# A hybrid RWKV-7 / S5 / PEER block on one core: the gather stream runs on through its two buffers instead of stopping at its tenth row

## The chip, the core and the metric

The kernel runs on one core of a Trainium2 chip. The core has a matrix engine (PE, with its weight loads shown as PEld), a vector engine (DVE), a scalar engine (ACT), a general engine (POOL) and a queue that issues plain transfers (SP). Each engine takes its instructions strictly in the order of the program. The metric is the device time of one execution in microseconds; lower is better.

## What is computed

One pre-norm residual layer over 1024 tokens of width 1024, in float32. Shortened:

```python
xn = rms_norm(x); p = xn @ w_in
y_a = rwkv7_time_mix(p[...])            # 8 heads x 64, a recurrence over the tokens
y_b = s5_ssm_glu(p[...])                # diagonal complex SSM, GELU, GLU
h = x + (sigmoid(g_a) * y_a + sigmoid(g_b) * y_b) @ w_out
# PEER, by blocks of 128 tokens: 8 heads, 16 of 128*128 single-neuron experts each
q = (xt @ wq); s = einsum(q, subkeys); sv, si = top_k(s, 16)
e, gate = best 16 of the 16 x 16 sums     # 128 experts for each token
hid = gelu(einsum('td,thkd->thk', xt, table_u[e]))
h = h + einsum('thk,thkd->td', gate * hid, table_v[e])
out = rms_norm(h)
```

## The kernel before

The tokens are eight blocks of 128. All blocks go through the projections, the S5 part, the RWKV recurrence and the mix into `h`; for the expert part they are split. Blocks 1 to 5 (`DB`) are **dense**: for them a gate table over all 16,384 experts is built with one-hot matmuls (tiles `oha`, `ohb`, `gm`, function `gate_table`), and then all experts are multiplied through, chunk by chunk of 128 experts (`dense_steps`: score matmuls into `S`, value matmuls into `acc`, weights `u` and `v` streamed from memory and split in high and low parts `uh`, `ul`, `vh`, `vl`). Blocks 0, 6 and 7 (`GB`) are **gathered**: for each of their 3 x 128 = 384 rows (one expert per token and row), POOL issues one indirect transfer of 128 x 2048 floats, a megabyte, into a buffer `row`. Then DVE takes the dot product with the token (`row<-row,gx`) and reads the sum out (`hid`), ACT takes the GELU and multiplies with the gate, and DVE adds the value half into the accumulator (`gacc<-row,hid,gacc`). The selection of a block (the `top16` and `combine` instructions `tv`, `ti`, `t`, `cv`, `ci`, `oh`) runs on DVE and partly on POOL. Blocks 6 and 7 (`LATE`) are selected only during the dense stage, in `late_steps`.

No order of instructions is written out. Fourteen streams (front, pre, state, mix, top, table, gather, dense, late and others, listed at line 2020) run as coroutines. A planner (`Weave`, lines 50 to 350) keeps a time line of its own for every engine with modelled durations, takes the operation that could start first by that time line, and among the operations that could start on that engine at that time the one with the highest bonus (`run`, line 260). The gather stream has the lowest bonus of the streams ahead of the dense stage, -1.0 (line 1994), so it gets the gaps that the planner sees. What the planner emits is the fixed order of each engine's program. Where an operation may go to DVE or POOL (`either`), the planner also chooses the engine.

The gather stream (`gather_stream`, line 1988) starts when block 0 is selected. At that time it has two `row` buffers. Until the flag `dense` it runs with `keep` = 1, that is, it takes the dot and the sum of row n-1 once row n is issued; after the flag it has a third buffer (later five), and it is spread evenly over the dense stage (`step`). At row number `GE` = 10 it waits for the flag `dense`, which the dense stream sets when the gate tables are complete (line 1964). The other flags are `mixed` (line 1898: the first six blocks are mixed; the table stream waits for it) and `tables`. Row 128 needs the selection of block 6.

Nearly all instructions are recorded on one line, L171, of the planner's `issue`; so the rows of the profile are told apart by their tiles.

Of the kernel before, what the change touches and what calls it, by code (L numbers as in the profile page):

```python
# [37 lines left out]
NG, ND = len(GB), len(DB)  # L38
# [336 lines left out]
class Kern:  # L375
# [1393 lines left out]
    def build(self, ctx, out):  # L1769
# [14 lines left out]
        NP = LATE[0] // 2  # L1784
        sc = [[] for _ in range(NP)]
        self.rings = {}
        GE = 10
        wv = self.weave
        E = mybir.EngineType
        X = {}  # L1790
# [197 lines left out]
        def gather_stream():  # L1988
            wv.wait(lambda: GB[0] in sel and "glu" in flags)
            wv.cur.kb = 2.0  # L1990
            self.padd, self.keep = 8, 1
            n, N, at, end = 0, 128 * NG, 0.0, 0.99
            RLT = 1.2
            wv.cur.bonus = -1.0
            for n in range(128 * NG + 1):
                if n == N:
                    break
                if n >= GE:
                    wv.wait(lambda: "dense" in flags)
                if "dense" in flags:  # L2000
                    self.padd = 0
                    self.keep = len(self.rings["row"]) - 1
                    step = (end - at) / (N - n)
                    if "late" not in flags:
                        step /= RLT
                    at = max(at + step, X["part"] - 2 * step)
                    wv.wait(lambda: X["part"] >= min(at, 2.0))
                b = GB[n // 128]
                wv.wait(lambda: b in sel)
                next(X["gs"])  # L2010
                X["early"] = n
            for _ in X["gs"]:
                pass

        with tc.manual_schedule(engines={E.Pool, E.Activation, E.DVE, E.PE, E.SP}):
            X["early"] = X["items"] = X["part"] = 0
            self.wp, X["xn"], X["gt2"] = self.pool(c1, "w1"), self.pool(c1, "xn"), self.pool(c1, "gt2")
            self.banks(c1, "ps1", 2, 0)
            X["sp"] = self.pool(c2, "s5p")
            S = dict(front=front_stream, pre=pre_stream, state=state_stream, mix=mix_stream, top=top_stream, table=table_stream,  # L2020
                     gather=gather_stream, dense=dense_stream, late=late_stream, norm=norm_stream, s5p=s5p_stream, s5=s5_stream, glu=glu_stream, split=split_stream)
            W = [int(i) for i in "100,100,100,100,100,100,60,250,100,100,100,100,100,100".split(",")]
            BO = [1.0, 1.0, 1.0, 2.8, 1.2, 2.0, -3.0, -2.0, 0.0] + [7.0, 1.0, 5.0] + [0.0, 0.0]
            wv.run(*((f, BO[i], W[i]) for i, f in enumerate(S.values())))
# [83 lines left out]
```

## Time and profile before

| | us |
|---|---|
| median of three runs | 3720.68 |
| lowest and highest of them | 3716.93, 3731.84 |
| the profiled execution's own time | 3725.95 |
| its span in the profile | 3723.9 |
| PE busy in the span | 3446.2 |
| DVE busy | 2757.2 |
| ACT busy | 1346.6 |
| POOL busy | 1191.9 |

The span is what the profile covers of the execution; some 2 us lie around it. Busy time is the sum over the engine's instructions. The kernel has stages with different limits, so the shares of the whole say little: the profile is read in stretches. By the tiles that are at work, the trace falls into: up to 1056 us (projections, S5, most of the RWKV recurrence; no gathered row is touched by DVE yet), 1056 to 1266 us (last mixes, selection of the blocks, RWKV, and the first gathered rows), 1266 to 1694 us (gate tables, with the end of RWKV), 1694 to 1800 us (the turn to the dense stage), and 1800 us to the end (dense stage with the gather; until about 2591 us with the late blocks 6 and 7 in it).

### The profile page before, as it was taken

Reading aid. Unit: us, or ns where it says so; the run is one execution under the profiler, and the core shown is the slowest. Engines: PE = TensorE matmul, PEld = TensorE weight load, DVE = VectorE, ACT = ScalarE, POOL = GpSimd, SP = SyncE. Lnnn points to the kernel's source line nnn. Section 1 sums busy time; section 2 is a strip of 40 time slices with the busy share of each in tenths; the row PEclk is TensorE's granted clock in tenths of the full one; section 3 lists DMA queues with packets and bytes.
Section 4 is the critical chain, followed back from the end, with each engine's and each line's share of the span. In section 5 each row is a group of like instructions: output and inputs, shape, how many; then the busy total and the mean of one; then the engine's idle time right before and its main releaser. Section 6 shows DMA issues by size and latency. Waiting matters only on the chain.

```text
span 3723.9 us, 59743 instructions
## 1 busy us (share of the span) xinstructions
PE 3446.2 (93%) x22415; PEld 2975.6 (80%) x22415; DVE 2757.2 (74%) x6150; ACT 1346.6 (36%) x2905; POOL 1191.9 (32%) x1137
## 2 busy tenths in 40 slices
PE   7989999999888999998998889988999999999997
PEld 7777687767666888897787778887989998888986
DVE  7555413546999967654788978888888888888888
ACT  4332323333232466663233323333333333333333
POOL 3653323532443344432222222122222222222221
PEclk9998999998889899899999899998999999999998
DMA  5641223355577422257888799877898988898886
GB/s 205 215 152 54 88 96 119 129 195 187 168 260 236 166 100 92 98 191 255 312 318 317 246 327 334 304 269 276 304 323 303 323 316 308 306 322 290 304 298 228
DMA packets 359953, 869.11 MB, mean 233 GB/s; under 512 B 28960, under 2 KB 175520, under 8 KB 307952
## 3 DMA queue, kind: packets, MB, share of 16 engines
q1 hardware_dynamic: 303792, 461.01, 36.8%
q0 software_dynamic: 55296, 402.68, 29.4%
q8 instruction: 176, 2.88, 0.3%
q10 hardware_dynamic: 576, 1.61, 0.1%
q14 instruction: 113, 0.93, 0.1%
HBM read 759.16 MB, written 104.86 MB: 232 GB/s over the span
## 4 chain that ended last, share of the span: by engine, by line
PE 48%; DVE 19%; issue 15%; DMA 10%; POOL 5%; ACT 2%; SPq 1%; POOLq 0%; DVEq 0%; ACTq 0%
PE S L171 11%; PE acc L171 10%; PE gm L171 9%; PE mm L171 7%; POOL row L171 5%; DMA G<-gd 3%; PE tps L171 3%; PE rs L171 2%; PE gl L171 2%; PE rw L171 2%; DVE gacc L171 2%; PE pp L171 1%; DMA row<-in_uv_dram,ei 1%; DMA w<-in_wout_dram 1%; DVE ti L171 1%
## 5 line engine op out<-in xcount | busy, mean ns | idle before, releaser
L171 POOL DMA_INDIRECT row<-in_uv_dram,ei x384 | 519.0, 1352 | 1499.2 <-DVE gacc L171 1253.4
L171 PE MATMUL S<-dx,uh 128*128 128x320 f32 x4096 | 790.4, 314 | 8.5 <-ACT w L171 6.1
L171 PEld LDWEIGHTS S<-dx,uh 128*128 128x128 f32 x4096 | 656.9, 190 | 27.9 <-ACT w L171 9.5
L171 PE MATMUL acc<-vh,wh 128*128 128x512 f32 x1280 | 504.3, 402 | 64.1 <-DVE acc L171 61.7
L171 DVE SCALAR_TENSOR_TENSOR gacc<-row,hid,gacc 128x1024 f32<-128x1024 f32 x384 | 491.2, 1279 | 71.7 <-ACT hid L171 71.1
L171 PE MATMUL acc<-vl,wh 128*128 128x512 f32 x1280 | 511.2, 399 | 11.2 <-DVE vl L171 11.0
L171 PE MATMUL acc<-vh,wl 128*128 128x512 f32 x1280 | 509.4, 398 | 0.1
L171 PE MATMUL S<-dx,ul 128*128 128x320 f32 x2048 | 478.4, 314 | 13.0 <-DVE ul L171 13.0
L171 DVE CUSTOM_DVE_ANT_0 row<-row,gx 128x1024 f32<-128x1024 f32 x384 | 468.3, 1220 | 18.1 <-DMA row<-in_uv_dram,ei 18.0
L171 PEld LDWEIGHTS S<-dx,ul 128*128 128x128 f32 x2048 | 346.8, 190 | 17.9 <-DVE ul L171 15.9
L171 PE MATMUL gm<-ohb,oha 128*128 128x128 f32 x1280 | 343.1, 430 | 5.5 <-ACT oha L171 5.0
L171 PEld LDWEIGHTS acc<-vh,wh 128*128 128x128 f32 x1280 | 244.0, 191 | 128.0 <-DVE acc L171 67.2
L171 PEld LDWEIGHTS gm<-ohb,oha 128*128 128x128 f32 x1280 | 311.3, 329 | 14.3 <-ACT oha L171 5.1
L171 PEld LDWEIGHTS acc<-vl,wh 128*128 128x128 f32 x1280 | 246.2, 192 | 61.4 <-DVE vl L171 15.5
L171 PEld LDWEIGHTS acc<-vh,wl 128*128 128x128 f32 x1280 | 245.7, 192 | 54.7 <-issue 1.7
L171 ACT ACTIVATE hid<-hid 128x1 f32<-128x1 f32 x384 | 77.2, 201 | 564.2 <-DVE hid L171 563.3
L171 ACT ACTIVATE vh<-vr 128x512 fp32r<-128x512 f32 x256 | 160.3, 627 | 284.2 <-PE acc L171 166.3
L171 DVE TENSOR_TENSOR acc<-acc,acc 128x512 f32<-128x512 f32 x320 | 213.0, 682 | 6.9 <-PE acc L171 6.4
L171 ACT ACTIVATE stg<-gm 128x512 f32<-128x512 f32 x160 | 172.5, 1079 | 119.2 <-PE gm L171 116.5
L171 POOL TENSOR_TENSOR ohb<-ohq,gT 128x512 f32<-128x512 bf16 x135 | 146.0, 1082 | 212.8 <-DVE ohq L171 116.1
L171 DVE TENSOR_TENSOR vl<-vr,vh 128x512 fp32r<-128x512 f32 x255 | 174.3, 685 | 52.4 <-ACT vh L171 52.1
L171 DVE TENSOR_TENSOR w<-w,G 128x640 f32<-128x640 f32 x128 | 105.1, 821 | 144.7 <-DMA G<-gd 114.3
(443 smaller groups left out, 6241.8 us busy)
## 6 DMA issues: line engine op xcount, KB each, us to landing
ur<-in_ut_dram SPq DMA_DIRECT2D x128, 512.0 KB, 6.5
vr<-in_uv_dram SPq DMA_DIRECT2D x256, 256.0 KB, 6.4
wf<-wsd SPq DMA_DIRECT2D x120, 512.0 KB, 5.5
gd<-stg SPq DMA_DIRECT2D x20, 2048.0 KB, 6.6
G<-gd SPq DMA_DIRECT2D x31, 1280.0 KB, 16.6
wsd<-sw SPq DMA_DIRECT2D x40, 512.0 KB, 3.4
wr<-in_wc_dram SPq DMA_DIRECT2D x30, 512.0 KB, 4.7
wr<-in_wg_dram SPq DMA_DIRECT2D x32, 256.0 KB, 3.3
```

What stands on the lines that cost most here:

```text
L171: op.alts = [(e, self.cost(e, n, outs, ins), lambda f=f, a=a, k=k: f(*a, **k)) for e, n, f, a, k in alts]
```

## The change

The constant `GE` and the wait at row `GE` are removed, and the loop is written more simply (the old loop also left at n = N). The order of everything else in the source is the same.

```diff
-        GE = 10
...
-            n, N, at, end = 0, 128 * NG, 0.0, 0.99
+            N, at, end = 128 * NG, 0.0, 0.99
             RLT = 1.2
             wv.cur.bonus = -1.0
-            for n in range(128 * NG + 1):
-                if n == N:
-                    break
-                if n >= GE:
-                    wv.wait(lambda: "dense" in flags)
+            for n in range(N):
                 if "dense" in flags:
                     self.padd = 0
                     self.keep = len(self.rings["row"]) - 1
```

Since the planner sets the order, the diff doesn't tell where instructions go. Counted in the programs of both kernels: 10 indirect transfers stand ahead of the gate tables and of the dense flag before; now 29 stand ahead of the tables, 32 more within them, and 61 in all ahead of the dense flag. The number of rows is 384 in both. In the text a row's place is told by the engine and by what stands near it.

**POOL, in the stretch with the last mixes and the RWKV steps, behind the tenth indirect transfer.** `abm`, `pb`, `Y`, `ar`, `bb` are masks and products of the RWKV steps, `ml` and `yx` are low parts for the mix. Before:

```order
L171 TENSOR_TENSOR pb_11745<-pb_11745,cst 128x512
L171 TENSOR_TENSOR Y_11746<-pb_11745,cst 128x256
L171 TENSOR_TENSOR abm_11919<-pb_11745,cst 128x256
L171 TENSOR_TENSOR Y_11746<-Y_11746,cst 128x256
L171 COPY rx_11884<-rtrn_11882 128x256
L171 TENSOR_TENSOR yx_12051<-h_12018,yx_12051 128x1024
```

Now:

```order
L171 TENSOR_TENSOR pb_11746<-pb_11746,cst 128x512
L171 DMA row_11916<-in_uv_dram,ei_10703 128x2048
L171 TENSOR_TENSOR Y_11747<-Y_11747,cst 128x256
L171 TENSOR_TENSOR abm_11920<-pb_11746,cst 128x256
L171 COPY rx_11883<-rtrn_11881 128x256
L171 DMA row_12031<-in_uv_dram,ei_10703 128x2048
L171 TENSOR_TENSOR yx_12041<-h_12008,yx_12041 128x1024
```

Further indirect transfers now stand between the RWKV and mix instructions; one of two `Y` products went over to DVE.

**DVE, up to the first one-hot compare of the gate tables (`oaq`, `ohq`).** `tv`, `ti`, `t` are the top-16 search of the selection, `X`, `m`, `ob`, `abm` belong to RWKV steps. Before:

```order
L171 MATCH_REPLACE t_13686<-tv_13120,sc_13553 128x128
L171 MAX_INDEX ti_13123<-tv_13122,t_13662 128x8
L171 MAX tv_13120<-t_13686 128x8
L171 TENSOR_TENSOR X_13652<-rx_13651,X_13143 128x256
L171 MAX_INDEX ti_13121<-tv_13120,t_13686 128x8
L171 MAX tv_13120<-sc_13553 128x8
L171 MAX tv_13122<-sc_13553 128x8
L171 MAX_INDEX ti_13121<-tv_13120,sc_13553 128x8
L171 TENSOR_TENSOR oaq_13718<-iotaM,iT_13712 128x512
L171 TENSOR_TENSOR ohq_13716<-iotaM,iT_13712 128x512
```

Now:

```order
L171 SCALAR_TENSOR_TENSOR gacc_10702<-row_14258,hid_14377,gacc_10702 128x1024
L171 TENSOR_REDUCE m_14387<-ob_14199 128x4
L171 MAX_INDEX ti_13889<-tv_13888,t_14450 128x8
L171 TENSOR_SCALAR m_14387<-m_14387 128x4
L171 MAX tv_13888<-sc_14098 128x8
L171 TENSOR_TENSOR ob_14199<-ob_14199,m_14387 128x256
L171 TENSOR_TENSOR X_14509<-rw_14508,X_14197 128x256
L171 TENSOR_TENSOR abm_14545<-pb_14195,cst 128x256
L171 TENSOR_TENSOR oaq_14528<-iotaM,iT_14522 128x512
L171 TENSOR_TENSOR ohq_14526<-iotaM,iT_14522 128x512
```

Ahead of the first `ohq` stand the dots and sums of 8 rows before and of 28 rows now, and 85 more instructions of RWKV and mix, while 42 instructions of the top-16 search (17 `tv`, 17 `ti`, 8 `t`) went behind it.

**PE, at the end of the gate tables.** Before:

```order
L171 MATMUL gm_17428<-ohb_17412,oha_17410 128x128 x4
L171 MATMUL S_17253<-dx_16757,ul_16932 128x320
L171 MATMUL S_17229<-dx_16757,uh_16931 128x320
L171 MATMUL gm_17442<-ohb_17431,oha_17429 128x128 x4
L171 MATMUL S_17229<-dx_16758,uh_16931 128x320
L171 MATMUL S_17253<-dx_16757,uh_16931 128x320
```

Now:

```order
L171 MATMUL gm_17885<-ohb_17868,oha_17866 128x128 x4
L171 MATMUL gm_17901<-ohb_17888,oha_17886 128x128 x4
L171 MATMUL gm_17914<-ohb_17904,oha_17902 128x128 x4
L171 MATMUL gm_17934<-ohb_17917,oha_17915 128x128 x4
L171 MATMUL acc_18006<-vh_16427,wh_17963 128x512
L171 MATMUL acc_18006<-vl_16428,wh_17963 128x512
```

The 192 score matmuls of the first four chunks now all stand within the tables; before, 107 of them stand behind the last `gm`.

## Rows read from the trace of the kernel before

**Rows 1.** The page's head: span, and each engine's busy time and share.

```profile
span 3723.9 us, 59743 instructions
PE 3446.2 (93%) x22415; PEld 2975.6 (80%) x22415; DVE 2757.2 (74%) x6150; ACT 1346.6 (36%) x2905; POOL 1191.9 (32%) x1137
```

**Rows 2.** Busy time by stretch: bounds and length in us, then each engine's busy us.

```profile
core 0: us, PE busy (x) PEld busy (x) DVE busy (x) ACT busy (x) POOL busy (x), PEclk, DMA share, GB/s
1056.00:1266.00 210.00, 172.90 (x1735) 146.98 (x1736) 197.59 (x872) 61.84 (x156) 71.52 (x72) 0.87 0.76 261
1266.00:1694.00 428.00, 412.76 (x2513) 377.87 (x2512) 280.60 (x786) 276.26 (x428) 183.81 (x162) 0.92 0.30 115
1694.00:1800.00 106.00, 85.42 (x478) 75.43 (x478) 58.17 (x81) 26.82 (x59) 20.51 (x15) 0.92 0.82 280
1800.00:2591.00 791.00, 720.35 (x3872) 630.20 (x3871) 673.92 (x1280) 244.65 (x596) 194.96 (x144) 0.95 0.85 302
2591.00:3668.00 1077.00, 1064.26 (x5931) 966.30 (x5930) 925.31 (x1231) 375.85 (x890) 292.04 (x215) 1.00 0.88 309
```

**Rows 3.** The chain that ended last, 1056 to 1266 us, its shares by line.

```profile
by line: DVE ti L171 10.5%; PE mm L171 8.2%; DVE tv L171 7.5%; issue 7.1%; DVE oh L171 7.0%; DVE t L171 6.4%; DMA wf<-wsd 3.7%; DVE ci L171 3.7%; DVE rtrn L171 3.3%; DVE rtrg L171 2.8%; DMA ga<-gad 2.7%; DVE cv L171 2.7%; PE rw L171 2.5%; P
```

**Rows 4.** The same chain, 1266 to 1694 us.

```profile
by line: PE gm L171 74.3%; PE rw L171 3.9%; PE rs L171 3.9%; PE S L171 3.3%; PE rx L171 2.7%; DVE oaq L171 1.7%; DVE oh L171 1.4%; ACT stg L171 1.3%; DVE ohq L171 0.8%; PE rm L171 0.8%; DVE ti L171 0.8%; issue 0.7%; ACT oha L171 0.6%; DVE t
```

**Rows 5.** Groups by form, whole span: count | busy us, mean ns | idle time before, releaser.

```profile
L171 POOL DMA_INDIRECT row<-in_uv_dram,ei x384 | 519.0, 1352 | 1499.2 <-DVE gacc L171 1253.4 <-DVE y L171 108.7 <-DVE ei L171 21.8
...
L171 DVE SCALAR_TENSOR_TENSOR gacc<-row,hid,gacc 128x1024 f32<-128x1024 f32 x384 | 491.2, 1279 | 71.7 <-ACT hid L171 71.1
...
L171 DVE CUSTOM_DVE_ANT_0 row<-row,gx 128x1024 f32<-128x1024 f32 x384 | 468.3, 1220 | 18.1 <-DMA row<-in_uv_dram,ei 18.0
...
L171 DVE TENSOR_TENSOR X<-rx,X 128x256 f32<-128x256 f32 x48 | 20.1, 418 | 32.4 <-PE rx L171 32.2
...
L171 PE MATMUL gm<-ohb,oha 128*128 128x128 f32 x1280 | 343.1, 430 | 5.5 <-ACT oha L171 5.0 <-issue 0.5
...
L171 DVE TENSOR_TENSOR oaq<-iotaM,iT 128x512 bf16<-128x512 bf16 x160 | 93.5, 584 | 121.3 <-ACT oha L171 112.7 <-ACT iT L171 7.9
```

**Rows 6.** DVE groups by form, 1056 to 1266 us.

```profile
L171 DVE FIND_INDEX8 ti<-tv,sc 128x8 uint32<-128x128 f32 x53 | 15.1, 284 | 0.0
...
L171 DVE MAX8 tv<-t 128x8 f32<-128x128 f32 x53 | 14.7, 278 | 0.1
...
L171 DVE CUSTOM_DVE_ANT_0 row<-row,gx 128x1024 f32<-128x1024 f32 x8 | 11.1, 1392 | 2.5 <-DMA row<-in_uv_dram,ei 2.5
L171 DVE SCALAR_TENSOR_TENSOR gacc<-row,hid,gacc 128x1024 f32<-128x1024 f32 x8 | 10.2, 1276 | 0.8 <-ACT hid L171 0.8
```

**Rows 7.** DVE time line: the ends of dense groups 1, 12 and 31.

```profile
1799.66 0.68 DVE L171 TENSOR_TENSOR acc<-acc,acc 128x512 f32<-128x512 f32 x1
...
2589.50 1.28 DVE L171 TENSOR_TENSOR acc<-acc,acc 128x512 f32<-128x512 f32 x2
...
3665.53 1.88 DVE L171 TENSOR_TENSOR acc<-acc,acc 128x512 f32<-128x512 f32 x3
```

**Rows 8.** Late blocks' projection (tile pp) in the dense stage: PE first after the length.

```profile
1800.00:2591.00 791.00, 81.84 (x428) 58.71 (x428) 4.42 (x8) 11.26 (x36) 0.95 0.85 302
```

**Rows 9.** Waits, 1800 to 2600 us: us in total, times, longest.

```profile
ACT hid L171 <- DVE hid L171: 246.5, 111, 7.4
```

**Rows 10.** DVE and POOL time lines: the first dot and POOL's instruction beside it; one stopped transfer.

```profile
1056.41 2.30 DVE L171 CUSTOM_DVE_ANT_0 row<-row,gx 128x1024 f32<-128x1024 f32 x1
...
1056.17 1.46 POOL L171 TENSOR_TENSOR pb<-pb,cst 128x512 f32<-128x512 f32 x1 [2.94 <-ACT pb L171]
...
1100.04 1.12 POOL L171 DMA_INDIRECT row<-in_uv_dram,ei  x1 [6.94 <-DVE gacc L171]
```

## The prediction

> **What bounds the kernel now.** I read the page's head first: PE is busy for 93% of the span and DVE for 74% [rows 1]. That is an average over stages with different limits, so I went to the table by stretch. From 1056 to 1266 us DVE is busy for 197.6 of 210 us, PE for 172.9: DVE has 12.4 us to spare. From 1266 to 1694 us it is the other way round: PE 412.8 of 428, DVE 280.6. From 1800 to 2591 us neither is full (PE 720 of 791, DVE 674), and from 2591 us on PE has 13 us of idle time in 1077, with DVE at 925 [rows 2]. The chain of waits agrees: in the first of these stretches its largest lines are the top-16 search and the one-hot work of the selection on DVE (`ti`, `tv`, `oh`, `t`, `ci`) [rows 3]; in the table stage 74% of it is the matmul `gm` [rows 4]. So the question is from which stretch vector work is taken, and into which it is put.
>
> **What the change moves.** Row counts come from the two programs. 51 of 384 rows go ahead of the dense stage. None is saved: a row still costs DVE 1.220 us for the dot and 1.279 for the sum, and POOL 1.352 us for the transfer [rows 5]. 20 of the 51 are computed ahead of the gate tables, about 31 within them.
>
> *Ahead of the tables.* Here the two DVE operations took 1.392 and 1.276 us [rows 6]; with the read-out of the sum, under 0.1 us, I take 2.75 us a row: 20 x 2.75 = 55 us. In the planner's new order 85 more RWKV and mix instructions also stand ahead of the first compare of the tables; priced kind by kind they come to 31 us, 0.36 us each (the product `X` with 0.418 [rows 5] is typical). Against that 42 instructions of the top-16 search, 0.28 us each [rows 6], went behind it: -12 us. Sum: 55 + 31 - 12 = +74 us of DVE work in front of a table stage that can't start without it. If it filled all of the 12.4 us of idle time, the stretch would grow by 62 us; if DVE kept its present 94%, by 79. I take **+70 us**. The cover that would make this free, idle DVE time, isn't there.
>
> *Within the tables.* A bank of `gm` for four tokens costs PE 343.1 / 160 = 2.14 us, and the stage takes 428 / 160 = 2.68 us a bank. DVE works 280.6 / 160 = 1.75 us a bank, and its compare `oaq` waited 112.7 us in all for the copy on ACT [rows 2, 5]. 61 more dots and sums are 76 us; less what RWKV leaves, DVE comes to some 2.1 us a bank, still under 2.68. So most of it is hidden by PE's work. It isn't hidden at two places: by the new order two sets of eight banks carry 34 and 30 us of DVE work, where eight banks take 21.4; before there is one such set, with 28. That is 13 + 9 - 7 = 15 us more. Part of the RWKV matmuls has left the stage (RWKV is some 11% of its chain [rows 4]), but the 107 score matmuls that stood behind the last `gm` have come in; PE's load hardly changes. I take **+10 us**, with -10 and +35 as ends: the upper one if every moved DVE operation holds PE for half a microsecond. The turn to the dense stage (1694 to 1800 us [rows 2]) I leave as it is: the score matmuls that leave it lay beside the transfers of the last table, so their leaving frees nothing.
>
> *In the dense stage.* I count groups of four chunks (ten sums into `acc`); the first of 32 ends at 1800 us, the twelfth at 2591 and the 31st at 3668 [rows 7]. Groups 2 to 12 take 791 / 11 = 71.9 us each with 673.9 / 11 = 61.3 us of DVE work; groups 13 to 31 take 1077 / 19 = 56.7 with 48.7 [rows 2]. The early ones also hold 81.8 / 11 = 7.4 us of PE work for the late blocks [rows 8]. So 12.6 us more of DVE work go with 15.2 us more time, of which 7.4 may be PE's: each microsecond of DVE is worth 0.62 to 1.21 us there. The programs have 283 gather operations in these eleven groups before and 247 now: 36 x 1.25 = 45 us less DVE work, worth 28 to 54 us; I take 41. In groups 13 to 31 it is 431 and 367, so 80 us less. But there PE is busy all but 13 us [rows 2], and no more than these can come back; I take 6. Together **-47 us**, between -28 and -67.
>
> The sum is 70 + 10 - 47 = **+33 us** on the profiled execution. Its own time is 3725.95 us, 5 us above the median of the three runs, with a span of 3723.9 [rows 1]. Set against the median: 3720.7 + 33 = 3754 us, 0.9% slower. The account in one line: 128 us of DVE work leave a stage where some 80 of them were hidden by PE, and most of it enters one where nothing hides it or one where it was not needed to.
>
> **A rule against the change.** The first dot lasted 2.30 us, where the usual is 1.22; POOL's mask product `pb` ran beside it, for 1.46 us [rows 10]. One long case of this size in 16 operations, 1.1 us, would be 7 us over the 102 moved ones; it is inside the ends above.
>
> The Trainium skill, "SBUF — State Buffer", section "Who interferes with whom", says that a DVE instruction with two SBUF inputs and a GpSimd instruction that reads SBUF block each other for a whole instruction. The dot and the sum have two such inputs, and in the dense stage POOL only issues transfers, whereas in the two earlier stretches it does products. With POOL busy about 40% of these, and half an instruction lost each time, an estimate by that page is some 20 us for the 102 operations; the sum would be +46 instead of +33. The trace agrees with the rule in one operation of 16 only, so I stay with the row.
>
> **The rivals.**
>
> *A. The early stretch isn't held by DVE, and the change gains.* DVE's lines that are shown make up about 44% of the chain from 1056 to 1266 us; the rest is PE, transfers and issue [rows 3]. If the added work fell into the waits of the other part, +74 would shrink to 74 x 0.44 = +32; with the dense stage at its better end, -67, and the tables unchanged, that is -35: 3686 us. It decides from where a microsecond taken from DVE in the dense stage brings back 1.2 us or more. For it: the early dense groups lose time that neither engine's busy time explains. Against it: DVE is 94% busy in the early stretch, and instructions that wait don't count as busy.
>
> *B. It comes out even.* With 62 ahead of the tables, nothing in them and 60 back, the sum is +2, some 3723 us. For it: all three values lie inside the ends that I gave. Against it: three ends at once.
>
> *C. The queues in front of the tables' own work.* ACT and POOL are in order too. ACT's GELU of a row waits for DVE's dot, in the dense stage 2.2 us a time (246.5 in 111) [rows 9]; behind it would now stand the copies `oha` and `stg`, for which DVE and PE wait. POOL's transfer waits for the sum that frees the buffer, once 6.9 us [rows 10], and behind it stands `ohb`. 31 rows x 2.2 us are 68 us; if 55 of them reach PE in place of my 10, the sum is +78: 3799 us. It decides when these waits outlast the buffers of the one-hot tiles, of which each has three, or 3 x 2.68 = 8 us of lead. Against it: most waits are shorter than that.
>
> *D. The change doesn't do what it says.* If the planner had kept the rows behind the tables, nothing would move; but 61 transfers stand ahead of the dense flag in the new program, so this is out.
>
> **How the numbers follow.** What a measurement of this kernel can tell from no change is about 0.5%, 18.6 us. My forecast, +33 with its own range from +10 to +65 us, gets 0.50; of this 0.12 lies under 18.6 us. A gets 0.17, B 0.13, C 0.20. So faster by more than 0.5%: 0.17. Within: 0.12 + 0.13 = 0.25. Slower: 0.38 + 0.20 = 0.58. The range reaches to A at the low end without its worst part, and to C at the upper: 3695 to 3802 us.
>
> **What would show it.** Right: the first `gm` starts 60 to 80 us later (about 1350 us), with DVE over 90% busy up to there; from first to last `gm` it takes 420 to 460 us; groups 2 to 12 take some 68 us each, 13 to 31 some 56.4; and the dense groups end about 30 us later than now. Wrong: the first `gm` is late by less than 40 us (A); the tables take 480 us, with ACT waiting for `hid` ahead of `oha` (C); or the early groups fall to 64 us or less, which would mean that DVE work there costs more than its own time.

## The result

The changed kernel takes 3755.9 us (median of seven runs, 3743.4 to 3762.0), the kernel before 3724.1 in the same comparison (seven runs, 3716.9 to 3734.0). The ratio is 1.0075, with a 95% interval from 1.0055 to 1.0096: **0.75% slower**, by some 31 us. The forecast was 3754 us. How far its terms were right is another matter: the sum came out, but three of its five terms were off by half or more, and a fourth was made up of two errors that cancelled.

First the head of the page of the changed kernel, to be set beside [rows 1]: the span, then each engine's busy time, share and instructions.

```profile
span 3754.5 us, 59704 instructions
PE 3438.6 (92%) x22415; PEld 2976.7 (79%) x22415; DVE 2796.4 (74%) x6138; ACT 1377.3 (37%) x2924; POOL 1214.4 (32%) x1144
```

The work is the same, yet DVE is busy for 39 us more, ACT for 31 and POOL for 23, in nearly as many instructions: most of them are the same, and some last longer. Next the busy time by stretch, with the bounds put at the same events as in [rows 2] (first row on DVE; first and last `gm`; ends of dense groups 1, 12 and 31):

```profile
core 0: us, PE busy (x) PEld busy (x) DVE busy (x) ACT busy (x) POOL busy (x), PEclk, DMA share, GB/s
1061.00:1342.00 281.00, 226.07 (x2540) 187.12 (x2540) 267.71 (x988) 107.83 (x272) 116.99 (x114) 0.85 0.76 270
1342.00:1786.00 444.00, 382.25 (x1812) 357.61 (x1812) 370.83 (x813) 285.31 (x443) 228.86 (x181) 0.80 0.50 185
1786.00:1882.00 96.00, 70.16 (x382) 62.41 (x383) 57.63 (x80) 22.00 (x51) 17.38 (x13) 0.85 0.85 303
1882.00:2641.00 759.00, 707.82 (x3846) 621.53 (x3845) 630.54 (x1225) 236.30 (x558) 186.68 (x126) 0.97 0.82 290
2641.00:3697.00 1056.00, 1055.05 (x5939) 963.99 (x5938) 851.74 (x1134) 364.19 (x824) 232.71 (x183) 1.00 0.81 283
```

In the first stretch DVE has 13 us to spare in 281, as it had 12 in 210. In the second PE has 62 us of idle time, where it had 15: PE isn't the only limit of the table stage any more. In the last stretch PE has 1 us, where it had 13.

The bounds of the table stage come from the row of the matmul `gm`: durations in ns (shortest, median, longest), then the first and the last start in us.

```profile
L171 PE MATMUL gm<-ohb,oha x1280: 407/416/604, 1344.2 to 1784.4; 128*128 128x128 f32 x183
```

In the kernel before:

```profile
L171 PE MATMUL gm<-ohb,oha x1280: 388/416/604, 1274.0 to 1693.4; 128*128 128x128 f32 x183
```

The chain of waits by line shows what holds the two stretches that grew, first 1061 to 1342 us, then 1342 to 1786, beside [rows 3] and [rows 4]:

```profile
by line: DVE gacc L171 8.9%; PE mm L171 7.6%; DVE row L171 7.3%; DMA row<-in_uv_dram,ei 6.9%; DVE oh L171 6.5%; issue 6.3%; DVE ti L171 6.2%; DVE tv L171 4.7%; DVE t L171 4.1%; DMA wf<-wsd 3.2%; DVE ci L171 2.6%; DVE rtrg L171 2.6%; DVE cv 
...
by line: PE gm L171 47.4%; DVE oaq L171 7.7%; ACT stg L171 4.9%; PE S L171 4.6%; DVE gacc L171 4.4%; DVE ohq L171 4.2%; DVE row L171 3.7%; issue 3.5%; DVE oh L171 3.0%; ACT oha L171 2.3%; DVE ohb L171 1.7%; DMA gd<-stg 1.7%; POOL ohb L171 1
```

Ahead of the tables the rows' sum (`gacc`), dot (`row`) and transfer now stand on the chain with 23% together; they had no share among the lines shown of [rows 3]. In the tables `gm` has fallen from 74% to 47%, and DVE's compares, sums and dots and ACT's copies have taken most of the rest.

Put together, in us (the turn is from the last `gm` to the end of dense group 1; each kernel's stretches are those of its one profiled execution, and a difference of 2 to 3 us is within what the starts differ by between runs):

| stretch | before | after | difference | forecast |
|---|---|---|---|---|
| first dot to first `gm` | 217.6 | 283.0 | +65 | +70 |
| first to last `gm` | 419.4 | 440.2 | +21 | +10 |
| the turn | 107 | 97 | -10 | 0 |
| groups 2 to 12 | 791 | 759 | -32 | -41 |
| groups 13 to 31 | 1077 | 1056 | -21 | -6 |

The rest of the 31 us is the start of the first dot (1061.2 us for 1056.4), the tail (1 us) and the rounding of the bounds.

### The profile page after: what moved, and what is told of

It is laid out like the page before. It is cut to its first block, busy times and chain, and to the rows that moved or that the text cites. A ratio compares the mean times of both kernels' runs of the same rounds, so it can differ in the third digit from the quotient of the medians.

```text
span 3754.5 us, 59704 instructions
## 1 busy us (share of the span) xinstructions
PE 3438.6 (92%) x22415; PEld 2976.7 (79%) x22415; DVE 2796.4 (74%) x6138; ACT 1377.3 (37%) x2924; POOL 1214.4 (32%) x1144
## 4 chain that ended last, share of the span: by engine, by line
PE 62%; DVE 21%; DMA 9%; issue 3%; ACT 3%; POOL 1%; SPq 1%; DVEq 0%; POOLq 0%; ACTq 0%
PE S L171 20%; PE acc L171 19%; PE mm L171 7%; PE gm L171 6%; PE tps L171 3%; DVE gacc L171 2%; PE gl L171 2%; DMA G<-gd 2%; DVE row L171 2%; PE rs L171 2%; DMA w<-in_wout_dram 2%; PE pp L171 2%; PE rw L171 1%; DVE oh L171 1%; DVE oaq L171 1%
## 5 line engine op out<-in xcount | busy, mean ns | idle before, releaser
L171 POOL DMA_INDIRECT row<-in_uv_dram,ei x384 | 507.1, 1320 | 1607.1 <-DVE gacc L171 1300.6
L171 DVE SCALAR_TENSOR_TENSOR gacc<-row,hid,gacc 128x1024 f32<-128x1024 f32 x384 | 502.4, 1308 | 53.9 <-ACT hid L171 53.4
L171 DVE CUSTOM_DVE_ANT_0 row<-row,gx 128x1024 f32<-128x1024 f32 x384 | 485.6, 1265 | 13.7 <-DMA row<-in_uv_dram,ei 7.4
L171 PE MATMUL gm<-ohb,oha 128*128 128x128 f32 x1280 | 335.0, 428 | 40.8 <-POOL ohb L171 13.7
L171 POOL TENSOR_TENSOR ohb<-ohq,gT 128x512 f32<-128x512 bf16 x132 | 160.1, 1217 | 166.5 <-DVE ohq L171 130.8
L171 ACT ACTIVATE w<-S 128x320 f32<-128x320 f32 x256 | 99.0, 434 | 284.3 <-PE S L171 278.7
```

Source lines behind the costliest of these rows:

```text
L171: op.alts = [(e, self.cost(e, n, outs, ins), lambda f=f, a=a, k=k: f(*a, **k)) for e, n, f, a, k in alts]
```

## The experiments

All edits are on the kernel before or on the changed one, and each diff says which lines differ. Stretches are named as in the table above. Ratios are to the kernel before, measured in the same comparison (medians of 3721.8 to 3724.1 us). An expectation gives a theory, and a rival that would show in another number.

**One row number instead of another.** The wait for the dense flag stays, at row 29 in place of 10: so the 19 rows that lie ahead of the tables move there, and the others stay behind the flag.

```diff
-        GE = 10
+        GE = 29
```

> The hold stands at row 29 instead of row 10: the stretch ahead of the gate tables has the same order as in the changed kernel (29 transfers), and no further row is gathered within the tables. Theory (DVE sets the stretch ahead of the tables, and this is the larger part of the loss): the first gm is as late as in the changed kernel, 70 us later than before; the tables take the 419 us of the kernel before or a little less; the dense stage has 38 gather operations less than before, not 101, and gives back about 20 us of the 53 that the changed kernel gets back. Sum +45 to +55 us on the kernel before, so slower than the changed kernel. Rival (the gather within the tables is the larger loss): +20 us or less.

Measured: 3731.2 us, ratio 1.0022 (0.9998 to 1.0045). The first `gm` is as late as in the changed kernel, 1341.3 us, but the table stage takes 384.8 us, 35 less than before, and the dense groups 779 and 1061. The theory's sum, +45 to +55, was wrong: it left out that the tables would shrink. So a part of the time ahead of the tables is only time that the tables lose to it: work that stood in the table stage was pulled ahead. That was not in my sum as a gain.

**Rows in the tables alone.** Row 10 and the next wait for the flag `mixed`, at which the table stream starts.

```diff
-                    wv.wait(lambda: "dense" in flags)
+                    wv.wait(lambda: "mixed" in flags)
```

> From row 10 on the stream waits for the flag of the mix instead of the dense flag: 10 transfers ahead of the tables as before, 27 within them. Theory: the first gm is where it is before; the tables take some 15 to 20 us longer (the changed kernel's tables, with 31 rows in them, took 21 longer); the dense stage with 53 operations less gives back about 28. Sum -15 to 0 us on the kernel before. Rival (the tables' lock step between ACT, DVE and PE pays for every row): tables 40 us longer, sum +12 us or more.

Measured: 3749.6 us, 1.0076 (1.0059 to 1.0093). The first `gm` stays where it was (1273.0) and the tables take 464.2 us, 45 more, with 27 rows in them: 1.7 us a row. The early groups gain nothing (797), the late ones 17 us (1059). The theory's 15 to 20 us for the tables was wrong and the rival's 40 was right. So rows in the table stage are dear, about as dear as ahead of it (27 to 31 us for 18 rows, below). "Most of it is hidden by PE's work" is wrong.

**The rows left out.** Rows 10 to 60 aren't fetched or computed; the order around them is that of the kernel before.

```diff
-                for f in (dot, gelu, weigh, add):
+                for f in (dot, gelu, weigh, add) if na in row else ():
...
-            if n < N:
+            if n < N and not 10 <= n < 61:
...
                 if n >= GE:
+                    self.keep = 200
+                if n >= 61:
                     wv.wait(lambda: "dense" in flags)
```

> Rows 10 to 60 of the gather are left out of the computation altogether (no transfer, dot or sum); the rest stands as in the kernel before up to the dense stage, and the dense stage has the 653 operations of the changed kernel. Theory: all the 50 to 55 us that the changed kernel got back in the dense stage (32 in its early groups, 21 in the later ones) come back here without the cost ahead of it: -50 to -62 us on the kernel before. Rival (the changed kernel's dense stage is quicker for another reason, such as its score matmuls standing earlier): -30 us or less.

Measured: 3668.1 us, 0.9849 (0.9829 to 0.9869). First `gm` 1280.7, tables 417.3, turn 92, groups 2 to 12 763, groups 13 to 31 1057. This is what the turn and the dense stage give back, with nothing added elsewhere: 56 us by the medians for 51 rows, 1.1 us a row. The dense groups of the changed kernel (759 and 1056) are within 4 us of these: that half of the account is complete.

**The order without the rows.** The changed program, in the planner's order to the instruction, but the five operations of rows 10 to 60 (transfer, dot, GELU, weight, sum) are planned and not emitted.

```diff
+            if 10 <= m < 61:
+                fn = lambda *a, **k: None
+            self.weave.issue((eng, name, fn, a, kw))
```

> The order of the changed kernel for everything else, but rows 10 to 60 are not emitted at all (no transfer, no vector work, no step on ACT: those rows are left out of the computation), so that only the other instructions' new places remain. The kernel that left the same rows out in the order of before took 3668 us. If the new order of RWKV, mix and selection by itself costs the time ahead of the tables: the first gm stays 45 us or more later than before (1274 us), and the tables take about 385 us. If the rows cost it: the first gm comes within 25 us of before. In both cases the tables tell what was left of 440 us when only the rows' vector columns went (413 us): 385 us would put the other 28 us on the rows' transfers and ACT steps, 410 us on the order.

Measured: 3675.5 us, 0.9873 (0.9829 to 0.9918). The row of `gm`:

```profile
L171 PE MATMUL gm<-ohb,oha x1280: 408/416/604, 1316.0 to 1717.1; 128*128 128x128 f32 x183
```

From the first dot to the first `gm` it takes 256.3 us: **39 of the 65 us that the change adds ahead of the tables come from the order alone**, with none of the 51 rows in it. (Two of the first ten rows, 8 and 9, are now computed ahead of the tables too, some 5 us of DVE work that stood behind them before; they count with the order.) The tables then take 401.1 us, 18 less than before. By the medians the new order costs 7 us (3675 for 3668 without the rows in the old order); the two intervals overlap, so its sign isn't settled. The busy times of the two stretches:

```profile
1060.00:1316.00 256.00, 217.22 (x2567) 180.70 (x2566) 224.84 (x937) 89.56 (x229) 89.04 (x95) 0.89 0.65 218
1316.00:1718.00 402.00, 371.84 (x1784) 355.33 (x1784) 265.42 (x714) 267.52 (x374) 173.75 (x150) 0.89 0.33 123
```

DVE is busy for 225 of 256 us here: 31 us idle, where the kernel before had 12. So the moved RWKV and mix work doesn't keep DVE full: it waits for the other engines (the largest of its waits there are for PE's `rm`, 5.2 us, ACT's `ob`, 3.9, and PE's `rs`, 3.2). The rows then fall partly into such gaps.

**The rows in the tables not emitted.** As above, for rows 28 to 60 only; those ahead of the tables are there.

```diff
+            if 28 <= m < 61:
+                fn = lambda *a, **k: None
+            self.weave.issue((eng, name, fn, a, kw))
```

> As the changed kernel, but only the rows within the tables, 28 to 60, are not emitted (left out of the computation); the 28 rows ahead of the tables stand. First gm as in the changed kernel (1344 us); tables of 385 us if the rows' own instructions make the 55 us, 410 us or more if the order does. Time: 55 us or more under the changed kernel by the first, about 35 by the second.

Measured: 3706.9 us, 0.9958 (0.9944 to 0.9973).

```profile
L171 PE MATMUL gm<-ohb,oha x1280: 398/416/604, 1341.1 to 1742.6; 128*128 128x128 f32 x183
```

First dot to first `gm` takes 286.2 us, tables 401.5: between the two values that I had expected, since the rows and the order both have a part. So the 18 rows ahead of the tables cost 27 to 30 us there (283.0 and 286.2 less 256.3) and 31 by the medians; the 33 within the tables cost 39 us there (440.2 less 401.5) and 49 by the medians.

That closes the account by medians: order +7, 18 rows +31, 33 rows +49, the dense stage -56: +31 us, the measured difference. It is closed by construction; what it shows is the sizes, and the intervals of these runs reach 5 to 17 us to either side.

**What of a row costs the time in the tables.** Two kernels have the order of the changed one with rows 28 to 60 altered. In the first the dot and the sum work on 64 of their 1024 columns; transfers, GELU and weight stay.

```diff
+            fn = real.tensor_tensor_reduce
+            if 28 <= m < 61:
+                fn = lambda **k: real.tensor_tensor_reduce(**{**k, "out": k["out"][:, :64], "in0": k["in0"][:, :64], "in1": k["in1"][:, :64]})
...
+            if 28 <= m < 61:
+                fn = lambda o, r, h, c, **k: real.scalar_tensor_tensor(o[:, :64], r[:, :64], h, c[:, :64], **k)
```

> The order of the changed kernel, instruction for instruction, but the dot and the sum of rows 28 to 60 (those within the tables) work on 64 columns (those rows' results are left out). Theory (DVE's time, lengthened by POOL's products beside it, costs the 55 us that the tables with rows take over the tables of the run with the hold at row 29): tables of 385 to 400 us instead of 440, the whole 35 to 55 us under the changed kernel. Rival (the waits of ACT and POOL in front of the one-hot copies cost it): tables of 425 us or more.

Measured: 3722.0 us, 1.0002 (0.9981 to 1.0022); the tables take 412.9 us.

```profile
L171 PE MATMUL gm<-ohb,oha x1280: 408/416/604, 1350.0 to 1762.9; 128*128 128x128 f32 x183
```

So of the 39 us for these rows 27 go with the columns of DVE's two operations, and 12 are what is left of a row (the transfer on POOL, ACT's two steps, the short operations). The shorter operations also shorten what waits for them: POOL's transfers wait 23 us for the sum in this stage, where the changed kernel's wait 35, and ACT's GELU 4 us for the dot, where it was 13. So the 27 aren't DVE's own time alone.

In the second they keep their 1024 columns but read one operand from SBUF (the on-chip memory in which most tiles lie) instead of two: a plain sum over the row's half.

```diff
+            if 28 <= m < 61:
+                fn = lambda **k: real.tensor_reduce(k["accum_out"], k["in0"], axis=AX.X, op=OP.add)
...
+            if 28 <= m < 61:
+                fn = lambda o, r, h, c, **k: real.tensor_reduce(h, r, axis=AX.X, op=OP.add)
```

> The order of the changed kernel, but the dot and the sum of rows 28 to 60 are replaced by plain sums over their 1024 columns, which read one operand from SBUF instead of two (those rows' results are left out). If the two inputs collide with POOL's products (in the changed kernel the dot took 1.70 us there and the sum 1.51, where 1.22 and 1.28 are usual, and POOL's ohb 1.22 instead of 1.08), these operations come to about 1.1 us, ohb back to 1.08 to 1.12, and the tables to 405 to 425 us. If the collision is with something else, the operations stay near 1.5 us and the tables at 435 us or more.

Measured: 3730.4 us, 1.0023 (1.0003 to 1.0043).

```profile
L171 PE MATMUL gm<-ohb,oha x1280: 408/416/603, 1347.1 to 1766.9; 128*128 128x128 f32 x183
```

The groups of DVE by form in the table stage of this kernel (count | busy us, mean ns | idle time before and what ended it):

```profile
L171 DVE TENSOR_TENSOR oaq<-iotaM,iT 128x512 bf16<-128x512 bf16 x159 | 99.8, 627 | 63.6 <-ACT oha L171 58.6 <-ACT iT L171 4.3
L1744 DVE TENSOR_REDUCE hid<-row 128x1 f32<-128x1024 f32 x32 | 38.8, 1213 | 17.6 <-ACT hid L171 17.5
L1728 DVE TENSOR_REDUCE hid<-row 128x1 f32<-128x1024 f32 x32 | 38.6, 1206 | 1.1 <-DMA row<-in_uv_dram,ei 1.1
```

The same in the changed kernel:

```profile
L171 DVE TENSOR_TENSOR oaq<-iotaM,iT 128x512 bf16<-128x512 bf16 x160 | 110.3, 690 | 54.0 <-ACT oha L171 48.6 <-ACT iT L171 4.9
L171 DVE CUSTOM_DVE_ANT_0 row<-row,gx 128x1024 f32<-128x1024 f32 x32 | 54.4, 1700 | 0.0
L171 DVE SCALAR_TENSOR_TENSOR gacc<-row,hid,gacc 128x1024 f32<-128x1024 f32 x31 | 46.6, 1505 | 9.1 <-ACT hid L171 9.1
```

A one-input sum over as many columns takes 1.21 us. The dot, 1.22 us over the whole kernel before [rows 5], takes 1.70 here, and the two-input sum 1.51 for 1.28. The tables take 419.8 us with the one-input sums and 440.2 with the two-input operations: **20 of the 39 us go with the second SBUF operand**, not with the length of the work. The compare `oaq` shows it too: 690 ns beside the two-input operations, 627 beside the one-input ones, 612 in the new order without the rows (584 before).

The one-input sums also write no result of 1024 columns, so this run alone leaves a rival: the output. The trace of the changed kernel speaks against it, by two operations on DVE that both write 128 x 256 floats. `abm<-pb,cst` reads both inputs from SBUF: started while a product ran on POOL it took 0.92 us in the mean of 6, and 0.41 without one (5 cases). `X<-rx,X` has one input that is a fresh result of PE: started while a product ran it took 0.42 us in the mean of 13, and 0.42 without one (28 cases).

**What the second operand runs into.** The time line of the changed kernel at the longest dot, DVE and POOL (start and length in us; in brackets the idle time before and what ended it):

```profile
1609.67 1.18 POOL L171 DMA_INDIRECT row<-in_uv_dram,ei  x1 [4.30 <-DVE gacc L171]
...
1610.52 5.27 DVE L171 CUSTOM_DVE_ANT_0 row<-row,gx 128x1024 f32<-128x1024 f32 x1
1610.88 3.81 POOL L171 TENSOR_TENSOR oh<-oh,If 128x1024 bf16<-128x1024 bf16 x2
```

The transfer had waited 4.3 us for the sum that frees its buffer; behind it two products had gathered on POOL, and they ran without a gap beside a dot that lasted over four times its usual 1.22. Of the 32 dots in the table stage 17 overlapped a product on POOL: 2.13 us in the mean. The other 15 took 1.22 us in the mean and none over 1.27. Of the 31 sums 24 overlapped (1.57 us), 7 did not (1.28). That is 17 x 0.91 + 24 x 0.29 = 22 us of longer DVE work. Of the 28 dots and 28 sums ahead of the tables 9 and 8 overlapped (1.59 and 1.79 us): another 8 us. POOL pays as well; its product `ohb` in the table stage, of the kernel before and then of the changed one:

```profile
L171 POOL TENSOR_TENSOR ohb<-ohq,gT 128x512 f32<-128x512 bf16 x135 | 146.0, 1082 | 212.8 <-DVE ohq L171 116.1 <-PE gm L171 51.2 <-ACT sa L171 12.7
```

```profile
L171 POOL TENSOR_TENSOR ohb<-ohq,gT 128x512 f32<-128x512 bf16 x132 | 160.1, 1217 | 166.5 <-DVE ohq L171 130.8 <-DVE rtrg L171 10.4 <-PE gm L171 9.9
```

From 1082 to 1217 ns: 18 us over 132; with the one-input sums it is back at 1078. And the cost arrives at PE: the idle time in front of `gm` grows from 5.5 us [rows 5] to 40.8, the largest shares of it behind POOL's `ohb`, no visible releaser ("issue") and DVE's `ohb`. Half of this growth, 18 us, is there without any row, in the new order alone. Its row of the changed kernel, then that of the order without rows:

```profile
L171 PE MATMUL gm<-ohb,oha 128*128 128x128 f32 x1280 | 335.0, 428 | 40.8 <-POOL ohb L171 13.7 <-issue 12.2 <-DVE ohb L171 9.5
```

```profile
L171 PE MATMUL gm<-ohb,oha 128*128 128x128 f32 x1280 | 327.3, 426 | 23.1 <-POOL ohb L171 6.9 <-DVE ohb L171 5.8 <-issue 4.8
```

The granted clock of the table stage falls with PE's waiting, from 0.92 [rows 2] to 0.80, a mean between the two levels of 1.2 and 2.4 GHz; but one `gm` takes 430 ns before and 428 after. Its busy time is 8 us above that without the rows, and PE's whole busy time in the stage 10 us (382 and 372). So the clock is a small part of the 39 us, 10 at most.

**What of a row costs the time ahead of the tables.** With the wait at row 29, the dot and the sum of rows 10 to 28 work on 64 columns.

```diff
+            if 10 <= m < 29:
+                fn = lambda **k: real.tensor_tensor_reduce(**{**k, "out": k["out"][:, :64], "in0": k["in0"][:, :64], "in1": k["in1"][:, :64]})
...
+            if 10 <= m < 29:
+                fn = lambda o, r, h, c, **k: real.scalar_tensor_tensor(o[:, :64], r[:, :64], h, c[:, :64], **k)
...
-        GE = 10
+        GE = 29
```

> The order of the run with the hold at row 29, instruction for instruction, but the dot and the sum of rows 10 to 28 work on 64 columns instead of 1024 (those rows' results are left out of the computation); transfers, ACT's steps and all waits stay. Theory (DVE's time sets the stretch ahead of the tables): about 19 x 2.35 = 45 us of vector work go, and the first gm comes 35 to 45 us earlier than in the run with the hold at row 29 (there 1341 us); the time falls to 25 to 40 us below the kernel before. Rival (POOL and ACT stopping in order for the rows, or the new order of the RWKV steps, cost the time): the first gm stays later than 1325 us and the time within 10 us of the kernel before.

Measured: 3721.8 us, 1.0006 (0.9989 to 1.0023). First dot to first `gm` takes 268.2 us, where full columns take 283.5. The stretch with full columns (wait at row 29), then with 64:

```profile
1058.00:1341.00 283.00, 228.30 (x2557) 188.42 (x2557) 267.67 (x1004) 108.50 (x271) 117.11 (x115) 0.86 0.76 267
```

```profile
1063.00:1331.00 268.00, 222.34 (x2557) 185.15 (x2557) 233.77 (x1005) 107.57 (x271) 109.79 (x116) 0.87 0.80 282
```

DVE's work fell by 34 us and the stretch by 15. Were DVE its only limit, all of it would have come back. The theory is wrong and the expectation's rival right (first `gm` at 1331 us, the time that of the kernel before). It is also rival A's mechanism of the prediction, with nearly A's own share: 0.45 us for each of DVE's, where A had 0.44.

**The rows as transfers alone.** With the wait at row 29, rows 10 to 28 are fetched and not computed.

```diff
-                for f in (dot, gelu, weigh, add):
+                for f in (dot, gelu, weigh, add) if not 10 <= na < 29 else ():
...
-        GE = 10
+        GE = 29
```

> As with the hold at row 29, but for rows 10 to 28 only the transfers are issued; their dots, GELUs, gate products and sums are left out of the computation. Theory (DVE's time is what the early rows cost ahead of the tables): the vector work ahead of the first compare is 30 us above that of the kernel before instead of 74 (the RWKV instructions have come ahead all the same), so the first gm comes 20 to 35 us later than before. Rival (the transfers, or POOL waiting with them, cost the time): the first gm comes 55 us or more later than before.

Measured: 3751.5 us, 1.0092 (1.0071 to 1.0114), and the first `gm` is later than with the dots, 1360.6 us. This run doesn't answer its question: without the dots between them the planner put the transfers close behind one another, from 1118 to 1203 us, and POOL stood 15 times until an earlier one had landed. Its waits from 1059 to 1360 us (in all, times, longest):

```profile
POOL row L171 <- DMA row<-in_uv_dram,ei: 37.4, 15, 6.0
PEld rx L171 <- POOL abm L171: 19.5, 4, 11.4
```

It does show the half of rival C's mechanism that concerns POOL: a transfer that waits stops POOL's queue, and PE waits for the masks (`abm`) that stand behind it.

**No row ahead of the dense stage.**

```diff
-        GE = 10
+        GE = 0
```

> No row is gathered ahead of the dense stage (hold at row 0). Theory (a row costs about 1.7 us ahead of the dense stage, and gives back 1.1 us there): faster than the kernel before by 10 x 0.6 = 6 us, between -12 and 0. Rival (the first ten rows filled gaps): 0 to +10 us.

Measured: 3764.6 us, 1.0121 (1.0084 to 1.0157), against the expectation. The first `gm` isn't earlier (1279.3): the first ten rows are free where the kernel before has them. Ten more rows in the dense stage cost 43 us by the medians, nearly four times for each what a row of the 51 gives back. Its stretches up to the first `gm` and for groups 13 to 31:

```profile
1059.00:1279.00 220.00, 182.37 (x1801) 153.22 (x1797) 189.28 (x894) 59.41 (x148) 57.04 (x58) 0.86 0.64 211
2599.00:3705.00 1106.00, 1071.92 (x5918) 968.13 (x5917) 941.86 (x1251) 377.22 (x900) 310.38 (x222) 0.98 0.87 307
```

The late groups take 1107 us, and PE is idle for 34 of them, 24 of these in front of value matmuls that wait for DVE's sum into `acc`:

```profile
L171 PE MATMUL acc<-vh,wh 128*128 128x512 f32 x757 | 294.6, 399 | 24.1 <-DVE acc L171 23.8
```

With ten rows ahead of the dense stage they take 1077, with 29 or more in every kernel 1055 to 1063: the first rows taken from the dense stage bring much there, the later ones almost nothing.

**Two more places for the wait.** The end of RWKV in place of the dense flag, which puts 9 rows at the end of the tables; and the dense flag at row 18.

```diff
-                    wv.wait(lambda: "dense" in flags)
+                    wv.wait(lambda: {"mixed", "rwkv"} <= flags)
```

> From row 10 on the stream waits until mix and RWKV are both done: 10 rows ahead of the tables as before, 9 at their end, where DVE has the most idle time. If a row in the tables costs 1.7 us wherever it stands: tables +15 us, dense stage -10, sum about +5 us on the kernel before. If the collisions and queues matter less there: tables +5, sum -5 us.

```diff
-        GE = 10
+        GE = 18
```

> The hold at row 18: 8 rows more than before ahead of the tables, none within them. With the run of 29 at +8 us, that of 10 at 0 and that of 0 at +40, a flat bottom is expected: -8 to +6 us on the kernel before. If the stretch ahead of the tables were paid by DVE's time alone it would be +8 x 1.6 = 13 us there, and the sum +5 or more.

Measured: 3734.6 us, 1.0044 (1.0027 to 1.0062), and 3738.0 us, 1.0048 (1.0025 to 1.0071). The first adds 10 us to the tables (429.0) and gains 16 in the late groups (1061); the early ones lose 6. The second has its first `gm` at 1314.0 us, tables of 403.3, and late groups that gain nothing (1081). Both were expected lower: the first between -5 and +5 us on the kernel before, the second in a flat bottom between rows 10 and 29; row 18 lies above row 10. With 19 rows ahead of the dense stage the one kernel has 1061 us in the late groups and with 18 the other 1081, so their number alone doesn't decide. No place that was tried (0, 10, 18, 29, in the tables, behind RWKV, no hold) beats the kernel before.

## Why the prediction was right, and where its steps failed

**Ahead of the tables, +70: +65 measured, for a partly different reason.** The first `gm` came at 1344 us (about 1350 forecast) with DVE at 95%. But the step "+74 us of DVE work in front of a table stage that can't start without it" put 55 us to the rows and 31, less 12, to the moved instructions. The runs show 27 to 31 us for 18 rows, and 39 for the order alone with the other two rows in it. The two errors cancelled, so it is luck that +70 came out so close. DVE's 94% did not mean that each microsecond added costs one: 34 us of it taken away gave back 15. The moved RWKV work cost more than its DVE time (DVE's work in the stretch grew by 27 us, two rows included, and the stretch by 39), since it comes with waits for the other engines.

**Within the tables, +10: +21 measured, as -18 and +39.** Both halves were missed. "PE's load hardly changes" was false: PE's instructions in the stage went from 2513 [rows 2] to 1812, and without the rows it shrank by 18 us, by 35 with the wait at row 29. And "most of it is hidden by PE's work" was false. I compared DVE's mean load per bank, 2.1 us, with PE's 2.68; but DVE, ACT and POOL make the next bank's operands in turn, each waiting for the other, and a mean doesn't say what one long operation holds up. The dot of 5.27 us stood in front of one-hot work of the selection (`oh`), and PE then waited 9.2 us for ACT's `slc`, which comes out of that work. The waits of the changed kernel's table stage show it, beside ACT's wait in [rows 9]:

```profile
ACT oha L171 <- DVE oaq L171: 53.9, 61, 6.5
DVE oaq L171 <- ACT oha L171: 48.6, 57, 3.6
POOL row L171 <- DVE gacc L171: 35.2, 17, 4.3
PEld gm L171 <- POOL ohb L171: 22.1, 25, 3.8
...
ACT hid L171 <- DVE hid L171: 12.7, 8, 4.8
```

Of the 39 us 20 go with the second operand of the rows' work. My own price for this was 7 us in all, left inside the ends and not added to the sum, from the single long dot of [rows 10], and "I stay with the row" was the wrong choice: the one case in sixteen came from a stretch where POOL was busy for 34% of the time, while in the tables of the changed kernel it is busy for 52%, with 17 of 32 dots and 24 of 31 sums beside a product.

The Trainium skill, "SBUF — State Buffer", section "Who interferes with whom", says that a DVE instruction with two SBUF inputs and a GpSimd instruction that reads SBUF keep each other out for an instruction at a time. The trace agrees: 17 dots beside a POOL product took 2.13 us in the mean, 15 others 1.22, and a one-input sum of the same width 1.21. The estimate of some 20 us from that page was for all 102 operations, in the tables and ahead of them; the trace has 22 us of longer DVE work in the tables alone and 8 ahead, so as a figure for that the estimate was low, but nearer than 7.

**The rivals.** C's mechanism (queues of ACT and POOL) is there, but not with its 55 us: POOL's transfers waited 35 us for the sum and ACT's GELU 13 for the dot. Of the 39 us 12 stay with DVE's operations cut to 64 columns and 19 with the one-input sums, where POOL still waited 34 us; C's part is not shown more closely than that. A's mechanism is there ahead of the tables, where 34 us of DVE work gave back 15, but A needed the dense stage to bring back 1.2 us or more for a microsecond of DVE: 51 rows are 128 us of DVE work and brought back 56, 0.44 us each.

**The turn, 0: -10 measured.** "Their leaving frees nothing" was about the score matmuls. The turn takes 92 us in the old order without the rows, 102 to 108 in the kernels with 19 rows or fewer ahead of it and 89 to 97 in the others, but not by the number of gathered rows in it: 13 of their dots fall into it before and 12 now, and 11 with no row ahead, where it takes 104 us. No run changed the turn alone; the cause stays open.

**Early groups, -41: -32 measured.** Inside its ends (28 to 54): 0.71 us for each of the 45 us of DVE work, nearer to the lower of the two prices, 0.62 and 1.21.

**Late groups, -6: -21 measured.** The step that failed is "PE is busy all but 13 us, and no more than these can come back". Of the 21 us 12 are idle time. The other 9 are busy time of PE itself: 1064 [rows 2] to 1055 us for as many matmuls. The score matmul in the last stretch, of the kernel before and then of the changed one, has 3 of them:

```profile
L171 PE MATMUL S<-dx,uh 128*128 128x320 f32 x2432 | 459.6, 311 | 5.3 <-ACT w L171 4.4 <-ACT uh L171 0.9
```

```profile
L171 PE MATMUL S<-dx,uh 128*128 128x320 f32 x2439 | 456.7, 309 | 0.9 <-ACT w L171 0.9
```

So a busy time can hold small delays that no row shows as idle; the profile models the ends of matmuls, and some of the 9 us may be idle time that it doesn't see. The chain of waits looks different too. Of the kernel before, 2591 to 3668 us:

```profile
by line: issue 42.0%; PE acc L171 17.5%; PE S L171 17.0%; POOL row L171 15.0%; DMA G<-gd 3.2%; DVE gacc L171 1.4%; DMA vr<-in_uv_dram 1.4%; DVE row L171 0.5%; DVE vl L171 0.4%; DVE ul L171 0.4%; ACT vh L171 0.3%; DVE acc L171 0.2%; DVE wl L
```

Of the changed one, 2641 to 3697 us:

```profile
by line: PE S L171 49.5%; PE acc L171 47.5%; DMA G<-gd 1.6%; issue 0.5%; DVE row L171 0.3%; DVE gacc L171 0.2%; DVE vl L171 0.1%; DVE ul L171 0.1%; ACT vh L171 0.1%; ACT hid L171 0.0%; ACT w L171 0.0%; SPq L171 0.0%; DVE wl L171 0.0%; DVE h
```

Before, the chain that ended last ran for its larger part over POOL's row transfers and the gaps between them ("issue", for which this view names no releaser), and PE had a third of it; afterwards PE has 97%. That looks as if POOL's transfers were a second limit, but two things speak against it. The waits of the same stretch of the kernel before say what POOL stood for, DVE's sum that frees a buffer:

```profile
POOL row L171 <- DVE gacc L171: 760.8, 211, 12.8
```

In the changed kernel, where PE has nearly the whole chain, POOL waits even longer for it (795 us of 1056). And PE's share of the chain doesn't go with the time. It is 86 to 100% in eight kernels whose late groups take 1055 to 1061 us, but 52% at 1060 (wait at row 29, 64 columns), 63% at 1059 (wait for `mixed`), 79% at 1063 (transfers alone), 52% at 1081 (wait at row 18) and 49% at 1107 (no row ahead).

What PE waits for points to DVE and ACT. Of the 12.7 us before, 4.4 end with ACT's `w` (above) and 5.2 with DVE's low part `ul`:

```profile
L171 PE MATMUL S<-dx,ul 128*128 128x320 f32 x1216 | 279.4, 311 | 5.3 <-DVE ul L171 5.2
```

With no row ahead 24 of 34 end with DVE's `acc`; in the changed kernel less than 1 us is left. DVE is busy for 942 us of the late groups with no row ahead, 925 before and 852 after the change. I take this as the reason why fewer rows brought time back in a stage that looked like PE's own, and why the gain ends at some 1055 us. It is argued, not shown: no run changed DVE's load in the late groups alone, and at the same 907 us of DVE work one kernel took 1061 us there (wait for RWKV) and another 1081 (wait at row 18). Where the 9 us of busy time come from stays open.

**The sum.** Term by term the misses are -5, +11, -10, +9 and -15 us, and some +8 lies outside the five stretches or in the rounding. That they leave 3754 us beside 3756 is luck; that the change loses, and that the loss ahead of the dense stage outweighs the gain in it, is not.

## What to carry to other kernels

Filler work on in-order engines is not free where an engine shows idle time: price it where it lands, by what waits behind it and by what runs beside it on POOL, not by the mean load of its engine. When a planner orders the program, test a moved piece of work in two runs, the new order without the work and the old order without it: here the order alone made more than half of the delay ahead of the tables and gave nearly half of that back within them. And an engine's idle time is not the most that can come back: here PE had 13 us of it in 1077, and 21 came back. Read what each of its waits ended with, and check a chain of waits against the wait rows before taking it at its word.

## What the hardware did that I had not expected

- A DVE operation with two SBUF operands of 128 x 1024 floats lasted up to 5.27 us, and 2.13 in the mean of 17, beside a product on POOL; 1.22 in the mean of 15 without one, and 1.21 for a one-input sum of the same width. An operation of which one input was a fresh result of PE wasn't lengthened: 0.42 us with a product running and without. The POOL product `ohb` went from 1.08 to 1.22 us in the mean in the same stage.
- 51 rows brought back 1.1 us each when they left the dense stage, but the ten rows that the kernel before has ahead of it cost 43 us when they were put in: over 4 us each.
- PE's busy time in the late groups fell by 9 us in 1064 with the same matmuls, at a granted clock of 1.00 in both.
